# The convolution's bias inside its band matrices, with 62-row window loads; LayerNorm's affine part on VectorE; modulation steps at 0.7 a unit

## The chip, the cores and the metric

The kernel runs on one core of a Trainium2 chip as one program. The core has a matrix engine (TensorE, PE in the profile), a vector engine (VectorE, DVE), an activation engine (ScalarE, ACT), a general engine (GpSimd, POOL), and a queue processor (SyncE, SP) that mostly issues transfers. Sixteen transfer engines move data between the chip's memory and the core's on-chip memory of 128 partitions (rows). Every engine works through its own instruction list in order, and waits on semaphores where an operand is not ready. The metric is the device time of one execution in microseconds.

## What is computed

The reference is one step of a two-layer backbone. 256 prompt tokens and 1024 sample tokens of width 1024 pass an even layer and an odd layer. The change touches the even layer. There the normalised input `h` is multiplied with one wide matrix, and the product is split into a gated convolution branch (`a_u`, `a_g`, `a_z`) and a differential attention branch (`b_q`, `b_k`, `b_v`, `b_z`):

```python
a_u, a_g, a_z, b_q, b_k, b_v, b_z = jnp.split(h @ w_in, SPLIT_E, axis=-1)
a = a_u * jax.nn.sigmoid(a_g)
a = lax.conv_general_dilated(a, conv_w[:, None, :], window_strides=(1,),   # 31 taps, one filter per channel
                             padding=[(15, 15)], ..., feature_group_count=A_W) + conv_b
a = jax.nn.silu(layer_norm(a, ln_g, ln_b)) * jax.nn.silu(a_z)              # A_W = 512 channels
```

`layer_norm` is `(x - mu) * rsqrt(var + 1e-6) * g + b` over the 512 channels. Attention follows with these queries, keys and values, then the output projection of both branches, then the odd layer. Each layer's input is shifted and scaled, and its output gated, by a modulation: `silu(cond) @ w_mod + b_mod`, a matrix of 1024 x 3072 per layer and two conditioning vectors.

## The kernel before

The program runs in stages: the first modulation and the normalised input, the even layer's input projection (`l0_in`, about 50 to 530 us), its attention (`l0_attn`, to about 810), its output projection, and the same for the odd layer.

**The input projection.** `l0_in` goes through seven groups of weight columns, 512 columns each, in the order `ug0`, `ug1` (the gated convolution input), `az`, and heads 0 to 3 (q, k, v and gate of one head each). A group has 10 or 14 units. A unit is 24 matmuls of three products (high and low parts of both sides) over eight slices of 128, into one bank of `acc` (5 buffers), and ends with a function that takes the result out on ACT and DVE and stores it to memory on SP's queue. The next group's eight weight slices (`raw_w`, `w_w`) are loaded in the group's last units, three ahead, cast on ACT and split on POOL (`wcut`).

**The convolution** is a side program, a Python generator `conv()` that `filler` advances by 4/3 steps after each unit. `ug_units` store the gated input, in high and low parts, to the memory tensors `AW` (a plane of rows of tokens per part, 256 channels wide, two buffers `ahl` on the way). For each of eight sets `q` of 64 channels, `windows(q)` (lines 432 to 440) loads `X`: 128 partitions, of which the first 64 hold the high part and the last 64 the low part of 64 successive token rows; 42 such windows with a step of 32 rows; 64 channels. A set takes four transfers, each of 64 rows with 21 pieces of 64 channels (256 bytes), issued on SP. `X` has two buffers, so set `q+2` can be loaded when set `q` has been used. A band matrix per channel (`toep`, two 256 KB loads in flight, cut by `wcut` on DVE) holds the 31 taps shifted 32 times: 64 rows, 32 columns, written twice one under the other. One matmul per channel (line 471, `tr_cv`) gives 42 x 32 output tokens; line 476 (ACT) and 477 (DVE) add the band's two parts into `cy`, and line 480 stores a set's `cy` to `CV` on ACT's queue, 42 rows of 32 pieces of 256 bytes. `AW` holds twice the gated value, so the result is twice the convolution without its bias.

**LayerNorm** follows as the second part of the same side program (`ln_steps`, 0.8 steps a unit), for ten tiles of 128 tokens: DVE halves and adds the bias (line 575), takes mean and variance (577 to 580), POOL raises to the power -1/2 (`rsq`, line 95), DVE makes the offset (582), ACT normalises (587), POOL multiplies by `ln_g` (588) and adds `ln_b` (589), ACT takes tanh (610), DVE applies both gates (593, 594), SP stores to `CAT`.

**The modulation** for later stages is a third side program, `mod_vec` (line 162): 48 steps, each a 256 KB load (`rawm`, two buffers) and two DVE operations of 128x512 that multiply and sum, each with a readout of the sum. `filler` advances it by one step a unit from the second group on.

**What sets the order.** The framework orders the instructions of each engine when the program is built, from the order written and from a model of times; on the chip each engine's list is fixed. `l0_in` calls `freed` six units before the end of the last head: the space of one input half is released, and the keys of attention head 0 and three query blocks are loaded there (`l0_keys`, `l0_query`, four loads of 128 KB each block). All SP transfers go through one hardware queue (q1), ACT's through another (q10), POOL's through a third (q0).

Of the kernel before, what the change touches and what calls it, by code (L numbers as in the profile page):

```python
# [76 lines left out]
class K:  # L77
# [323 lines left out]
    def l0_in(self, ws, raw, wp, cxp, p1, small, acc, pst, mod, freed):  # L401
# [21 lines left out]

        def conv():

# [6 lines left out]
            def windows(q):  # L432
                x = cxp.tile([128, CWIN, CCH], F32R, tag="X", bufs=2, name=f"X{q}")
                cs = slice(q % 4 * CCH, q % 4 * CCH + CCH)
                for o in range(2):
                    for hl in range(2):
                        src = self.AW[q // 4][hl, 32 * o : 32 * o + 32 * CWIN, cs].rearrange("(j r) c -> r j c", r=64)
                        dst = x[hl * 64 : hl * 64 + 64].rearrange("p (j o) c -> p o j c", o=2)[:, o]
                        nc.sync.dma_start(f32(dst), f32(src))
# [43 lines left out]
        def head_units(h):  # L483
# [23 lines left out]
            def vz_done(t, ps):  # L507
                v = small.tile([128, 128], F32, tag="vz", name=f"vz{h}_{t}")
                nc.scalar.copy(v, ps[:, 256:384])
                nc.sync.dma_start(self.V0[h, t], v)  # L510
                gz = small.tile([128, 128], F32, tag="gz", name=f"gz{h}_{t}")
# [45 lines left out]
        def ln_steps():  # L557
# [3 lines left out]
            con = cxp.tile([128, 3, 512], F32, tag="cy", bufs=1, name="lncon")  # L561
            for i, nm in enumerate(("lng", "lnb", "convb")):
                nc.sync.dma_start(con[:, i], a[nm].broadcast_to([128, 512]))
# [9 lines left out]
            def stats(t):  # L573
                u = us[t % 6]
                nc.vector.scalar_tensor_tensor(u, u, 0.5, con[:, 2], ALU.mult, ALU.add)
# [4 lines left out]
                nc.vector.tensor_scalar(mv[:, 1:2], mv[:, 1:2], EPS, None, ALU.add)  # L580
                self.rsq(mv[:, 2:3], mv[:, 1:2])
                nc.vector.tensor_scalar(mv[:, 3:4], mv[:, 0:1], mv[:, 2:3], -1.0, ALU.mult, ALU.mult)

            def norm(t):
                u, mv = us[t % 6], mvs[t]
                nc.sync.dma_start(azs[t % 2], self.AZ[t])
                nc.scalar.activation(u, u, AF.Identity, bias=mv[:, 3:4], scale=mv[:, 2:3])
                nc.gpsimd.tensor_tensor(u, u, con[:, 0], ALU.mult)
                nc.gpsimd.tensor_tensor(u, u, con[:, 1], ALU.add)
# [25 lines left out]
        convd, credit, RATE, LNR = [], [0.0], 4 / 3, 0.8  # L615
# [9 lines left out]
        def filler(rate, mods, at=None):  # L625
# [5 lines left out]
            def f(b):  # L631
# [4 lines left out]
                for _ in range(b):  # L636
# [4 lines left out]
                    for _ in range(mods):  # L641
# [6 lines left out]
            (1, lambda: ug_units(1), tok, filler(RATE, 1)),  # L648
            (6, az_units, tok, filler(RATE, 1)),
            (2, lambda: head_units(0), hd, filler(RATE, 1)),  # L650
            (3, lambda: head_units(1), hd, filler(RATE, 1)),
            (4, lambda: head_units(2), hd, filler(RATE, 1)),
            (5, lambda: head_units(3), [1] * 14, filler(RATE, 1, 6)),
# [929 lines left out]
```

## Time and profile before

| | |
|---|---|
| Median of 3 runs | 1825.25 us (1824.95 to 1827.32) |
| The profiled execution's own time | 1827.64 us |
| Its span, first to last instruction | 1825.9 us |
| PE busy | 1727.1 us (95%) |
| DVE / ACT / POOL busy | 1242.8 / 974.1 / 797.3 us |
| Transfers | 241.24 MB, mean 132 GB/s |
| Convolution matmuls (line 471) | 512 groups, 139.2 to 405.0 us |
| LayerNorm's operations | 423.7 to 499.2 us |
| Granted TensorE clock, mean | 0.985 |

The profile is one execution. The rows of a stage table give, for a stretch of time in us from the span's start, its length, then the busy time (and number of instructions) of PE, PE's weight loads, DVE, ACT and POOL, then the granted TensorE clock, the mean share in which the sixteen transfer engines had packets under way (overlapping packets count twice, so it can be over 1), and GB/s. A row of a wait table names who waited, for whom, the total in us, how often, and the longest. A row of a tile's table gives shortest, median and longest duration in ns, then first and last start in us. A row of the transfer table gives KB of one transfer and the median us from issue to landing.

### The profile page before, as it was taken

The page shows a single profiled execution, that of the slowest core. Times are in us where ns is not written, and L with a number is a line of the kernel's source. Part 1 is how long each engine was busy: PE and PEld are TensorE (multiplying, and loading weights), DVE is VectorE, ACT ScalarE, POOL GpSimd, SP SyncE. Part 2 cuts the span into 40 slices and gives each one's busy share as a digit, 9 for nine tenths or more (in the row PEclk, how much of TensorE's full clock was granted, in tenths as well). Part 3 has the DMA queues.
Part 4 walks back from the last instruction along what each step waited for, and adds up shares of the span by engine and source line. Part 5 has one row for each costly group of instructions (what it writes and reads, how often), then busy time and mean ns, then how long its engine had stood idle before and what let it go on. Part 6 is the DMA issues. An engine that isn't in the chain of part 4 may idle for free. (4 is left out here: it accounts for less than half of the span.)

```text
span 1825.9 us, 28267 instructions
## 1 busy us (share of the span) xinstructions
PE 1727.1 (95%) x9434; PEld 1421.5 (78%) x9434; DVE 1242.8 (68%) x2935; ACT 974.1 (53%) x2060; POOL 797.3 (44%) x716
## 2 busy tenths in 40 slices
PE   6998999998979899999999999998999999999998
PEld 2787788887767677778887778877888888878886
DVE  7656665675859889935576672118999899999322
ACT  6432334443347678743344533227778788898311
POOL 2321032236637777863237873202343334455332
PEclk9999999999989999999999999999999999999999
DMA  8468878865693332144246345254122114141441
GB/s 299 160 157 196 214 208 185 205 178 167 182 254 93 101 100 88 45 138 162 76 158 194 140 132 156 81 141 103 36 57 58 30 41 107 59 137 61 154 172 58
DMA packets 220278, 241.24 MB, mean 132 GB/s; under 512 B 72128, under 2 KB 154848, under 8 KB 219876
## 3 DMA queue, kind: packets, MB, share of 16 engines
q1 hardware_dynamic: 207476, 233.53, 44.2%
q0 software_dynamic: 1792, 3.15, 0.9%
q10 hardware_dynamic: 10864, 2.75, 0.8%
q8 instruction: 75, 1.23, 0.3%
q14 instruction: 71, 0.58, 0.1%
HBM read 169.08 MB, written 70.28 MB: 131 GB/s over the span
## 5 line engine op out<-in xcount | busy, mean ns | idle before, releaser
L397 ACT ACTIVATE E<-E,mm 128x1536 f32<-128x1536 f32 (+3 forms) x240 | 293.1, 1224 | 71.1 <-DVE E L394 61.4
L270 POOL TENSOR_TENSOR w_w<-raw_w,w_w 128x512 fp32r<-128x512 f32 x88 | 122.9, 1406 | 246.3 <-ACT w_w L269 232.8
L1239 PE MATMUL S<-k1d,q1s 128*128 128x512 f32 (+1 forms) x704 | 206.0, 390 | 4.8 <-DVE E L394 2.1
L372 POOL TENSOR_TENSOR el<-ef,eh 128x512 fp32r<-128x512 f32 x96 | 124.1, 1293 | 188.2 <-DVE eh L371 183.3
L394 DVE TENSOR_SCALAR_CACHE_REDUCE E<-S,mm 128x512 f32<-128x512 f32 x256 | 190.0, 744 | 14.8 <-PE S L799 5.2
L1169 PE MATMUL wt_et<-ident,E 128*128 128x128 f32 x1264 | 187.4, 273 | 3.7 <-DVE om L1192 2.3
L1169 PEld LDWEIGHTS wt_et<-ident,E 128*128 128x128 f32 x1264 | 154.8, 141 | 39.2 <-DVE om L1192 2.7
L368 DVE TENSOR_TENSOR el<-wt_et,eh 128x512 fp32r<-128x512 f32 x220 | 147.0, 682 | 8.3 <-ACT eh L367 7.9
L1239 PEld LDWEIGHTS S<-k1d,q1s 128*128 128x128 f32 x704 | 120.3, 190 | 27.2 <-DVE E L394 7.9
L1164 PE MATMUL pv_pv<-el,v 128*128 128x512 f32 x316 | 139.1, 440 | 0.4 <-POOL el L372 0.2
L367 ACT CAST eh<-wt_et 128x512 fp32r<-128x512 f32 x220 | 123.6, 592 | 26.8 <-PE wt_et L1169 26.2
L799 PE MATMUL S<-kd,qs 128*128 128x512 f32 (+1 forms) x416 | 130.0, 426 | 7.6 <-DVE E L394 6.3
L319 PE MATMUL acc_g<-w_w,hi 128*128 128x512 f32 x336 | 132.3, 394 | 0.0
L318 PE MATMUL acc_g<-w_w,hi 128*128 128x512 f32 x336 | 131.5, 393 | 0.8 <-DVE v L1022 0.7
L320 PE MATMUL acc_g<-w_w,lo 128*128 128x512 f32 x336 | 131.7, 392 | 0.0
L1163 PE MATMUL pv_pv<-eh,v 128*128 128x512 f32 x316 | 128.2, 406 | 0.6 <-DVE eh L371 0.3
L874 PE MATMUL acc_po<-wo,oh 128*128 128x512 f32 x320 | 126.2, 396 | 0.3 <-DVE oy L746 0.3
L875 PE MATMUL acc_po<-wo,oh 128*128 128x512 f32 x320 | 125.2, 392 | 0.0
L394 DVE TENSOR_SCALAR_CACHE_REDUCE E<-S 128x512 f32<-128x512 f32 (+1 forms) x160 | 100.1, 630 | 17.3 <-PE S L1239 9.2
L269 ACT CAST w_w<-raw_w 128x512 fp32r<-128x512 f32 x96 | 58.9, 619 | 94.4 <-DMA raw_w<-in_we 29.5
L878 PE MATMUL acc_po<-wo,ol 128*128 128x512 f32 x320 | 103.2, 394 | 0.0
L799 PEld LDWEIGHTS S<-kd,qs 128*128 128x128 f32 x416 | 70.3, 196 | 28.6 <-DVE E L394 20.4
(295 smaller groups left out, 4570.7 us busy)
## 6 DMA issues: line engine op xcount, KB each, us to landing
rawm_v<-in_wmodt SPq DMA_DIRECT2D x64, 256.0 KB, 3.1
raw_w<-in_we SPq DMA_DIRECT2D x56, 256.0 KB, 3.1
X<-AW SPq DMA_DIRECT2D x32, 336.0 KB, 7.1
qs<-QK SPq DMA_DIRECT2D x80, 128.0 KB, 2.8
ac<-CAT SPq DMA_DIRECT2D x20, 512.0 KB, 4.1
raw_w<-in_wod SPq DMA_DIRECT2D x40, 256.0 KB, 2.6
q1s<-qT SPq DMA_DIRECT2D x40, 256.0 KB, 2.6
xraw_m<-in_wmod SPq DMA_DIRECT2D x32, 256.0 KB, 4.4
```

What stands on the lines that cost most here:

```text
L318: nc.tensor.matmul(ps[:, o:], a, w[:, 0, o:], start=(k == 0), stop=False)
L319: nc.tensor.matmul(ps[:, o:], a, w[:, 1, o:], start=False, stop=False)
L320: nc.tensor.matmul(ps[:, o:], b, w[:, 0, o:], start=False, stop=(k == KC - 1))
L368: nc.vector.tensor_tensor(lo, ps, f32(hi), ALU.subtract)
L394: nc.vector.tensor_scalar(e[:, o : o + w], S, -1.0, init, ALU.mult, ALU.min, accum_out=m[:, i : i + 1])
L397: nc.scalar.activation(e[:, :n], e[:, :n], AF.Exp, bias=init, scale=-1.0, accum_out=s)
L799: nc.tensor.matmul(S, q[:, hl], kd[:, c, kofs + o : kofs + o + n], start=(hl == 0), stop=(hl == 1))
L874: nc.tensor.matmul(po[hn], oh[:, k, :], wo[k][:, 0, s], start=(k == 0), stop=False)
L1163: nc.tensor.matmul(pv, vs, wh, start=(i == 0), stop=False)
L1164: nc.tensor.matmul(pv, vs, wl, start=False, stop=(i == nk - 1))
L1169: nc.tensor.transpose(ps[:, g * 128 : g * 128 + 128], E[g][:, ec : ec + 128], self.ident)
L1239: nc.tensor.matmul(S, qs[:, g, :], kd[hl][:, kc : kc + n], start=(hl == 0), stop=(hl == 1))
```

## The change

- **Window loads and the bias.** The two window tiles are allocated once (`win`) and partly filled by POOL: rows 32 to 63 with 2.0 and rows 96 to 127 with 0.0, four fills of 32 x 2688 numbers. The loads then write 62 rows of each half in place of 64, so rows 62 and 63 keep 2.0 and 126 and 127 keep 0.0. Row 62 of every band matrix, zero until now, holds the channel's bias. The matmul so adds twice the bias. The number of loads (32), of their pieces per row (21) and their issuing queue stay.
- **LayerNorm.** Line 575 and the offset of 582 go, since the bias is in, and the factor 2 is left in and met by `4 * EPS`. Normalising and the affine part are two DVE operations: `(u - mean) * g`, then `* rstd + b`. ACT's operation and POOL's two a tile go.
- **Modulation** steps run at 0.7 a unit in place of 1.
- **Buffers.** `vz` and `gz`, a unit's value and gate on their way to memory, get three buffers in place of two.
- **Queries.** One query block of head 0 is loaded ahead in place of three; the others are loaded by the attention stage when it gets to them.

```diff
+        win = [cxp.tile([128, CWIN, CCH], F32R, tag="X", bufs=2, name=f"win{i}") for i in range(2)]
+        for w in win:
+            nc.gpsimd.memset(f32(w[32:64]), 2.0)
+            nc.gpsimd.memset(f32(w[96:128]), 0.0)
...
             def windows(q):
-                x = cxp.tile([128, CWIN, CCH], F32R, tag="X", bufs=2, name=f"X{q}")
+                x = win[q % 2]
                 cs = slice(q % 4 * CCH, q % 4 * CCH + CCH)
                 for o in range(2):
                     for hl in range(2):
-                        src = self.AW[q // 4][hl, 32 * o : 32 * o + 32 * CWIN, cs].rearrange("(j r) c -> r j c", r=64)
-                        dst = x[hl * 64 : hl * 64 + 64].rearrange("p (j o) c -> p o j c", o=2)[:, o]
+                        src = self.AW[q // 4][hl, 32 * o : 32 * o + 32 * CWIN, cs].rearrange("(j r) c -> r j c", r=64)[0:62]
+                        dst = x[hl * 64 : hl * 64 + 62].rearrange("p (j o) c -> p o j c", o=2)[:, o]
                         nc.sync.dma_start(f32(dst), f32(src))
...
-                v = small.tile([128, 128], F32, tag="vz", name=f"vz{h}_{t}")
+                v = small.tile([128, 128], F32, tag="vz", bufs=3, name=f"vz{h}_{t}")
...
-                gz = small.tile([128, 128], F32, tag="gz", name=f"gz{h}_{t}")
+                gz = small.tile([128, 128], F32, tag="gz", bufs=3, name=f"gz{h}_{t}")
...
             def stats(t):
                 u = us[t % 6]
-                nc.vector.scalar_tensor_tensor(u, u, 0.5, con[:, 2], ALU.mult, ALU.add)
...
-                nc.vector.tensor_scalar(mv[:, 1:2], mv[:, 1:2], EPS, None, ALU.add)
+                nc.vector.tensor_scalar(mv[:, 1:2], mv[:, 1:2], 4 * EPS, None, ALU.add)
                 self.rsq(mv[:, 2:3], mv[:, 1:2])
-                nc.vector.tensor_scalar(mv[:, 3:4], mv[:, 0:1], mv[:, 2:3], -1.0, ALU.mult, ALU.mult)
...
             def norm(t):
...
-                nc.scalar.activation(u, u, AF.Identity, bias=mv[:, 3:4], scale=mv[:, 2:3])
-                nc.gpsimd.tensor_tensor(u, u, con[:, 0], ALU.mult)
-                nc.gpsimd.tensor_tensor(u, u, con[:, 1], ALU.add)
+                nc.vector.scalar_tensor_tensor(u, u, mv[:, 0:1], con[:, 0], ALU.subtract, ALU.mult)
+                nc.vector.scalar_tensor_tensor(u, u, mv[:, 2:3], con[:, 1], ALU.mult, ALU.add)
...
-        convd, credit, RATE, LNR = [], [0.0], 4 / 3, 0.8
+        convd, credit, RATE, LNR, MR = [], [0.0, 0.0], 4 / 3, 0.8, 0.7
...
-                    for _ in range(mods):
+                    credit[1] += mods
+                    while credit[1] >= 1:
+                        credit[1] -= 1
                         next(mod, None)
...
-                pre.extend([[p], k.l0_keys(0, p, 1), {g: k.l0_query(0, g, p, 3) for g in (1, 2, 0)}])
+                pre.extend([[p], k.l0_keys(0, p, 1), {1: k.l0_query(0, 1, p, 1)}])
...
+    band[:, 62] = i["a_conv_b"][0][:, None]
```

The order of SP's transfers at the first window sets, before (a number behind a name is a buffer's; `x4` is four instructions alike; `AW<-ahl` are stores of the second group's units, `rawm` loads of the modulation, `rawb` loads of bands):

```order
L261 DMA rawm_v_2_5_0_1416<-in_wmodt 128x512
L439 DMA X_1135<-AW_73 64x21x64 x4
L439 DMA X_1281<-AW_73 64x21x64 x2
L420 DMA AW_74<-ahl_2_1131 128x2x256
L439 DMA X_1281<-AW_73 64x21x64
L420 DMA AW_74<-ahl_3_1184 128x2x256
L439 DMA X_1281<-AW_73 64x21x64
L261 DMA rawm_v_2_6_0_1481<-in_wmodt 128x512
```

And there in the change:

```order
L261 DMA rawm_v_2_4_0_1539<-in_wmodt 128x512
L445 DMA win_739<-AW_73 62x21x64 x4
L445 DMA win_740<-AW_73 62x21x64 x4
L263 DMA raw_w_0_1476<-in_we 128x512
L263 DMA raw_w_1_1478<-in_we 128x512
L263 DMA raw_w_2_1480<-in_we 128x512
L261 DMA rawm_v_2_5_0_1602<-in_wmodt 128x512
L261 DMA rawm_v_2_6_0_1722<-in_wmodt 128x512
L420 DMA AW_74<-ahl_2_1137 128x2x256
L420 DMA AW_74<-ahl_3_1178 128x2x256
```

The eight loads of the first two sets now stand together; the stores of units 2 and 3, which stood among them, come behind them, with three weight slices and two modulation loads in between.

SP at the third window set, in the change (before, the set stood at the same place, with `raw_w_5` and one band load among its four):

```order
L263 DMA raw_w_4_1508<-in_we 128x512
L445 DMA win_739<-AW_73 62x21x64 x4
L263 DMA raw_w_5_1522<-in_we 128x512
L263 DMA rawb_band_1590<-in_toep 128x512
L261 DMA rawm_v_0_7_0_2422<-in_wmodt 128x512
L261 DMA rawm_v_1_0_0_2539<-in_wmodt 128x512
L263 DMA raw_w_6_1554<-in_we 128x512
L263 DMA raw_w_7_1568<-in_we 128x512
```

The last three weight slices of the next group (`az`) stand behind the set, as do the next band and two modulation loads.

VectorE at the start of LayerNorm, before:

```order
L575 SCALAR_TENSOR_TENSOR lnw_4291<-lnw_4291,lncon 128x512
L340 SCALAR_TENSOR_TENSOR gz_5_4391<-th_z_5_4392,acc_v_5_4363 128x128
L577 BN_STATS bn_4399<-lnw_4291 128x6
L575 SCALAR_TENSOR_TENSOR lnw_4291<-lnw_4291,lncon 128x512
L513 TENSOR_TENSOR gz_5_4391<-gz_5_4391,subg 128x128
L579 BN_AGGR mv_4401<-bn_4399 128x2
```

And in the change, a little further on, where the first modulation operation stands among LayerNorm's:

```order
L592 SCALAR_TENSOR_TENSOR lnw_4189<-lnw_4189,mv_4357,lncon 128x512
L584 BN_AGGR mv_4457<-bn_4455 128x2
L584 BN_AGGR mv_4505<-bn_4503 128x2
L597 SCALAR_TENSOR_TENSOR lnw_4189<-lnw_4189,lnw_4190 128x512
L162 ISA md_v_1_2_1_0_4775,modv_1_1184<-rawm_v_1_2_1_4773,cr(0, 2)_1_3255 128x512
L162 ISA modv_1_1184 128x1
L500 TENSOR_TENSOR ch_2_1_4346<-cn_2_1_4392,ropeT 128x512
```

Before, the last modulation operation stood ahead of LayerNorm's first. Now twelve of them stand between its first statistics and its last store, and the two DVE operations of the affine part stand where ACT's and POOL's results were awaited.

More of the change, by code (lines that the diff above doesn't have):

```diff
@@ L557, in ln_steps @@
         def ln_steps():
-            con = cxp.tile([128, 3, 512], F32, tag="cy", bufs=1, name="lncon")
-            for i, nm in enumerate(("lng", "lnb", "convb")):
+            con = cxp.tile([128, 2, 512], F32, tag="cy", bufs=1, name="lncon")
+            for i, nm in enumerate(("lng", "lnb")):
                 nc.sync.dma_start(con[:, i], a[nm].broadcast_to([128, 512]))
@@ L647, in l0_in @@
             (0, lambda: ug_units(0), [4, 1, 1, 1, 3], filler(0, 0)),
[L648 to L653, printed above, removed]
+            (1, lambda: ug_units(1), tok, filler(RATE, MR)),
+            (6, az_units, tok, filler(RATE, MR)),
+            (2, lambda: head_units(0), hd, filler(RATE, MR)),
+            (3, lambda: head_units(1), hd, filler(RATE, MR)),
+            (4, lambda: head_units(2), hd, filler(RATE, MR)),
+            (5, lambda: head_units(3), [1] * 14, filler(RATE, MR, 6)),
         ]
@@ L1524, in _layout @@
         band[:, m : m + 31, m] = i["a_conv_w"][0].T
+    band[:, 62] = i["a_conv_b"][0][:, None]
     band = band.reshape(32, 16, 64, 32).transpose(0, 2, 1, 3).reshape(32, 64, 512)
     z["toep"] = c(np.concatenate([band, band], 1))
-    z["convb"] = c(i["a_conv_b"])
     z["lng"], z["lnb"] = c(i["a_ln_g"]), c(i["a_ln_b"])
```

## The prediction

> **What bounds the kernel now.** I read the page's first part, then one row of the stage table for the stretch in which the convolution's windows are loaded, then the waits of TensorE in that stretch.
>
> ```profile
> span 1825.9 us, 28267 instructions
> PE 1727.1 (95%) x9434; PEld 1421.5 (78%) x9434; DVE 1242.8 (68%) x2935; ACT 974.1 (53%) x2060; POOL 797.3 (44%) x716
> 128.00:352.00 224.00, 216.45 (x1334) 184.79 (x1333) 141.04 (x294) 80.41 (x183) 46.19 (x30) 0.99 0.84 199
> PE tr_cv L471 <- DVE cy L477: 6.0, 4, 4.0
> PE tr_cv L471 <- DMA X<-AW: 1.9, 1, 1.9
> ```
>
> The kernel is TensorE's: 1727.1 of 1825.9 us, and 216.45 of the 224 us in which it works on the projection and the convolution together. In that stretch it waited 1.9 us, once, for a window (`X<-AW`, columns: time, times, longest). The windows are free now. But the transfer engines are 0.84 busy there, so nothing says that they stay free when they get slower.
>
> **The window loads: how many engines carry one.** This is the edit that decides. Each of the 32 loads moved 64 rows (partitions) of 21 pieces of 256 B; now it moves 62 rows. I looked up in the transfer table on how many of the 16 engines loads with odd numbers of rows ran.
>
> ```profile
> DMA packets 220278, 241.24 MB, mean 132 GB/s; under 512 B 72128, under 2 KB 154848, under 8 KB 219876
> q0 software_dynamic: 1792, 3.15, 0.9%
> q10 hardware_dynamic: 10864, 2.75, 0.8%
> X<-AW SPq DMA_DIRECT2D x32, 336.0 KB, 7.1
> CV<-cy ACTq DMA_DIRECT2D x8, 336.0 KB
> AW<-z SPq DMA_DIRECT2D x2, 98.0 KB
> AW<-z SPq DMA_DIRECT2D x2, 30.0 KB, 3.6
> qn<-in_qn SPq DMA_DIRECT2D x1, 32.0 KB
> modc<-in_bmodc SPq DMA_DIRECT2D x4, 4.0 KB, 3.1
> ```
>
> Queue q10 carries only the eight stores `CV<-cy` of 42 rows by 32 pieces of 256 B, 10,752 packets; 10,864 were counted. The other 112 are 14 a store: one closing packet from each engine that took part. So 42 rows ran on 14 engines, three rows each. Two rules fit that: only equal shares are dealt out (14 is the largest divisor of 42 up to 16), or shares are rounded up (three rows each, until they run out). For 62 rows the first gives 2 engines with 31 rows each, the second 16 engines with four or fewer.
>
> The page's count of short packets separates them. Of 72,128 under 512 B, 43,008 are window pieces (32 x 64 x 21), 10,752 are `CV` pieces, 256 belong to `qn` and `kn`, 256 to `cc` and `bcol`, and 1,280 to the ten 4 KB column loads like `modc`. That leaves 16,576 closing packets. SP issues 1,016 transfers (all its counts in the issue table), ACT 8, POOL 16; 16 apiece would be 16,640. So 64 are missing. The `CV` stores miss 16. Two transfers of 2 rows (`condr`) miss 28, two of 15 rows (the 30 KB `AW<-z`) miss 2. The last 18 must be the two 49-row transfers (98 KB: 49 rows of two 1 KB pieces): 9 missing each, 7 engines. With shares rounded up these would use 13 engines and miss 6 in all. 7 is the largest divisor of 49 up to 16: equal shares it is, and a 62-row load runs on **two engines**.
>
> The Trainium skill has this as a rule: "DMA: Bandwidth & Descriptors", section "Why a DMA increments its semaphore by 16 and not by 1", says that a hardware-queue transfer uses the largest number of engines up to 16 that divides the outermost size of both sides. It speaks against this change; the trace agrees, with 14 for 42 rows and 7 for 49.
>
> **What one load then costs.** Each of the two engines moves 31 x 21 = 651 pieces of 256 B instead of 84.
>
> ```profile
> 130.00:132.00 2.00, 2.00 (x10) 1.60 (x9) 2.00 (x8) 0.97 (x3) 0.00 (x0) 1.00 1.24 215
> 134.00:136.00 2.00, 2.00 (x11) 1.59 (x10) 0.00 (x0) 0.00 (x0) 0.00 (x0) 1.00 1.38 171
> 530.00:540.00 10.00, 8.18 (x24) 5.11 (x24) 9.02 (x27) 7.28 (x10) 2.71 (x3) 0.83 1.10 326
> 127.93 9.45 SPq L439 DMA_DIRECT2D X<-AW  x6
> 141.86 0.58 SPq L439 DMA_DIRECT2D X<-AW  x1
> 172.22 5.68 SPq L439 DMA_DIRECT2D X<-AW  x3
> 353.36 2.01 SPq L439 DMA_DIRECT2D X<-AW  x2
> ```
>
> The last figure of a stage row is GB/s over 16 engines. Windows alone are in flight at 130 (215 GB/s, one engine 13.4, 19.1 ns a piece) and at 134 (171 GB/s, 24.0 ns). By queue q10, 0.8% of 16 x 1825.9 us over 10,864 packets is 21.5 ns. Below all of these lies the rate for large pieces at 530, 326 GB/s: 20.4 GB/s an engine would be 12.5 ns. Two engines load memory far less than sixteen, so I take 20 ns, near the 19.1 row. Four loads make a window set, and all four use the same two engines: 4 x 651 x 20 ns = **52.1 us a set** (49.7 at 19.1, 62.5 at 24, 32.6 at 12.5), where it was 4 x 84 x 20 ns = 6.7 us.
>
> **What waits for it.** There are eight sets, the first two issued together at 127.93 to 141.86, each later one when the set before last has been consumed (172.22 is the third). Every SP transfer that is spread over the engines has a sixteenth on each of the two busy ones, behind the window pieces in the same queue. The order of SP shows weights, the `AW` stores, `rawm` and band loads right behind each set; none of them finishes before it. TensorE goes on until it needs one of these. The stores' tiles (`ahl`, `az`, `ch`) have two buffers, so I let it run two units.
>
> ```profile
> 412.57 0.39 PE L330 MATMUL acc_c<-hi,w_w 128*128 128x512 f32 x1
> 418.07 0.39 PE L330 MATMUL acc_c<-hi,w_w 128*128 128x512 f32 x1
> ```
>
> The two rows are 24 matmuls apart, one unit: 5.5 us, two are 11.0. The first pair of sets adds 2 x 52.1 - 11.0 = 93.2 us, each of the other six 52.1 - 11.0 = 41.1, together 246.6. Sum **+340 us**. As a cross-check, the busiest engine's own work: 8 x 52.1 = 417 us of windows; the rest of the stretch is 199 GB/s x 224 us = 44.6 MB, less 30 windows (10.3 MB) and six `CV` stores (2.1 MB), 32.2 MB, a sixteenth at 20.4 GB/s 99 us, and 11 us for `CV`. That is 527 us for what took 233 (127.93 until the last set lands 7.1 us after 354): at least +294.
>
> **The other edits.** They meet in the LayerNorm stage and are small beside this.
>
> ```profile
> 430.00:440.00 10.00, 3.80 (x16) 2.65 (x15) 10.00 (x20) 4.57 (x10) 9.29 (x7) 0.77 0.14 33
> 450.00:460.00 10.00, 6.88 (x37) 5.55 (x36) 8.07 (x10) 3.59 (x9) 10.00 (x8) 0.96 0.67 211
> 500.00:520.00 20.00, 14.66 (x83) 13.24 (x83) 5.49 (x12) 5.50 (x24) 5.05 (x4) 0.83 0.95 257
> PE acc_v L318 <- DVE gz L340: 5.5, 1, 5.5
> L588 POOL TENSOR_TENSOR lnw<-lnw,lncon x10: 1262/1736/1747, 431.2 to 483.6; 128x512 f32<-128x512 f32 x10
> L587 ACT ACTIVATE lnw<-lnw,mv x10: 804/816/827, 429.9 to 481.9; 128x512 f32<-128x512 f32 x10
> L593 DVE SCALAR_TENSOR_TENSOR lnw<-lnw,lnw x9: 682/1573/1784, 436.4 to 493.5; 128x512 f32<-128x512 f32 x9
> L162 DVE CUSTOM_DVE_ANT_0 md_v<-rawm_v,cr(0, 2)_1_2586 x48: 680/700/1784, 218.1 to 395.6; 128x512 f32<-128x512 f32 x48
> L405 POOL MEMSET z<- x1: 515/515/515, 0.9 to 0.9; 64x512 f32 x1
>   DMA GZ<-gz: 6.6, 4
> ```
>
> TensorE idles 6.2, 3.1 and 5.3 us in the three rows, 14.6 us, the most that can be won here. One wait of 5.5 us is on `gz`, which stands on VectorE behind LayerNorm's work. VectorE's own 128x512 operation takes 682 ns alone and 1573 in the middle, where POOL is 9.3 to 10 of 10 us busy. POOL loses 20 operations (ten at 1.7 us; the ten of line 589 are like them), ACT ten of 0.82 us, VectorE gains ten of 0.68 less ten small ones, some 5 us. The third buffers of `vz` and `gz` take away the 6.6 us that VectorE waited for `GZ` stores, on a busy engine four times. Against it stand 12 modulation operations at 0.70 us, 8 us, which the order of VectorE puts into the LayerNorm rows. I take -8 for these (bounds -15 and 0). The four fills of the window tiles are 32x2688 on POOL, no row shows one; by `z` (512 columns in 515 ns) 2.7 us each, 0 to 10.8. I take 0, since they stand before the windows' wait and POOL is empty there (0.00 in the rows at 130 and 134). The queries: eight loads fewer before the attention, the same eight behind its start, 0 (-5 to 5).
>
> Sum: 340 - 8 = +332 on the profiled span of 1825.9; that execution took 1827.6, 2.4 us over the median of the runs, so 1825 + 332 = **2157 us**.
>
> **The rivals.**
>
> A, as above: two engines, partly covered. Range 2085 (the engine's own work at 19.1 ns a piece, +275, less 15) to 2240 (24 ns a piece, 83 us more). Chance 0.62.
>
> B, nothing is covered: VectorE's next modulation operation or band cut waits for a load behind the windows, and the convolution's own evictions (`cy`) stand behind it, so TensorE stops at once. For it: `DVE cy` is already what TensorE waits for most in this stretch (6.0 us). Against it: two band and two `rawm` loads are in hand at any time. At 24 ns: 8 x 62.5 = 500, less 8: 2317 us. Chance 0.20.
>
> C, the two engines are quicker when alone: 12.5 ns, as for large pieces. For it: 215 GB/s falls to 171 when more windows are in flight, so something shared limits sixteen engines. Against it: small pieces cost more per byte in every row here. 93.2 becomes 54.2 and 41.1 becomes 21.6: +184 - 8, 2001 us. Chance 0.12.
>
> D, 62 rows still run on 16 engines, some with a row less; then the windows are 3% smaller and only the small edits count: 1825 - 8 = 1817 us, faster. It decides if this path deals rows out differently from the 49-row transfers. Against it: the closing packets. Chance 0.05. Something else: 0.01.
>
> **How the numbers follow.** 2157 is A's time. The range 2000 to 2340 takes in A and most of B and C; D and their edges are left out. A measurement of this kernel can tell about 0.2% from no change. Only D is not slower: faster 0.04, same 0.01, slower 0.95.
>
> **What would show it.** In the new profile the loads `win<-AW` should land some 50 us after issue or later, not 7. TensorE should stand idle some 330 us more, nearly all between 130 and 700 us, released by transfers or by VectorE and ACT operations that waited for transfers; the share of busy transfer engines there should fall from 0.84 to below 0.5. Queue q1's packets should fall by 32 x 42 pieces and 32 x 14 closing packets. Attention and the second layer should keep their lengths to some 5 us. If the windows still land in under 15 us, D holds. If the sets land in 33 us, C; if TensorE does nothing while a set is in flight, B. In the LayerNorm stage POOL should be less than half as busy and VectorE's operations nearer to 0.68 us.

## The result, and the profile after

| | before | after |
|---|---|---|
| Median of 4 runs, us | 1825.78 (1824.95 to 1827.32) | 2031.48 (2029.30 to 2038.96) |
| Ratio of the runs | | 1.1123, interval 1.1104 to 1.1141 |
| Profiled execution, us | 1827.64 | 2029.30 |

The change makes the kernel about 206 us slower. The forecast was 2157 us, 332 us slower, with a range from 2000 to 2340 us. The measured time is in the range, but below the 2085 to 2240 us that the prediction's own account, A, gave, and nearest to the 2001 us of its rival C.

The first view is the page of the changed kernel: the span, the busy time of the engines, TensorE's busy tenths in 40 slices of 50.7 us, and the main transfer queue.

```profile
span 2027.5 us, 28257 instructions
PE 1743.0 (86%) x9434; PEld 1431.5 (71%) x9434; DVE 1217.8 (60%) x2935; ACT 964.5 (48%) x2050; POOL 775.6 (38%) x700
PE   6963665673958989999999989999899999999998
q1 hardware_dynamic: 205540, 232.92, 38.0%
```

TensorE is at 3 to 7 tenths from the third slice to the tenth and in the twelfth (101 to 608 us), and at 8 or 9 from then on. Queue q1 has 1,936 packets fewer: 32 x 42 pieces, 32 x 14 closing packets, and 144 that belong to the load of the bias vector that is gone (128 pieces and 16 closing packets). The first two terms are those that the prediction named for loads on two engines.

The next view is the table by stage, before (first fence) and after (second). The first row of each is the whole stretch from the first window load to attention's first matmul, the second lies inside the convolution, and the third runs from the last convolution matmul to attention.

```profile
128.00:526.00 398.00, 373.71 (x2310) 323.99 (x2309) 256.51 (x512) 144.90 (x357) 128.15 (x91) 0.97 0.77 194
172.00:405.00 233.00, 226.47 (x1476) 196.86 (x1475) 152.41 (x314) 92.38 (x219) 56.47 (x38) 0.99 0.82 201
405.00:526.00 121.00, 105.10 (x615) 92.64 (x615) 75.32 (x135) 40.17 (x112) 65.40 (x50) 0.92 0.66 184
```

```profile
124.00:737.00 613.00, 397.45 (x2319) 340.38 (x2318) 244.64 (x516) 137.46 (x349) 98.25 (x72) 0.81 0.45 126
230.00:623.00 393.00, 244.63 (x1474) 210.10 (x1473) 132.39 (x274) 91.18 (x219) 54.09 (x38) 0.79 0.40 113
623.00:737.00 114.00, 103.25 (x600) 90.50 (x600) 83.28 (x179) 33.19 (x101) 37.88 (x31) 0.94 0.73 210
```

The stretch grew from 398 to 613 us, by 215; it starts about 3 us earlier, and attention behind it is 10 us shorter. TensorE's idle time in it grew from 24.3 to 215.6 us, by 191, and its busy time by 24. In the middle rows nearly the same number of matmuls (1,476 and 1,474) takes 393 us in place of 233, while the transfer engines fall from 0.82 to 0.40 busy. The last rows went the other way, from 121 to 114 us.

What the two engines do is seen at the first sets, in rows of 5 us of the changed kernel.

```profile
140.00:145.00 5.00, 0.00 (x0) 0.00 (x0) 0.00 (x0) 0.00 (x0) 0.00 (x0) 0.50 0.16 36
160.00:165.00 5.00, 0.12 (x2) 0.15 (x3) 0.00 (x0) 0.00 (x0) 0.00 (x0) 0.50 0.16 36
165.00:170.00 5.00, 5.00 (x28) 4.11 (x28) 2.30 (x4) 1.95 (x4) 0.00 (x0) 0.63 0.16 36
170.00:175.00 5.00, 5.00 (x33) 4.20 (x32) 0.00 (x0) 0.96 (x2) 0.00 (x0) 1.00 0.15 33
```

At 140 us no engine of the core does anything. The transfer engines move 36 GB/s at a share of 0.16 of sixteen, which is 2.5 engines' worth, as overlapping packets count twice. The rows of the kernel before at 130 and 134 us had 215 and 171 GB/s. 36 GB/s over two engines is 18 GB/s an engine, 256 bytes in **14.2 ns**. The prediction had taken 20 ns. A set is 4 x 651 x 14.2 ns = 37.0 us, not 52.1. The rows also show the granted clock: 0.50 in the last 5 us of the idle time, 0.63 in the first 5 us of work after it, then 1.00.

The waits of TensorE (first fence, 100 to 760 us) and of VectorE (second, 100 to 620 us) in the changed kernel:

```profile
PE tr_cv L477 <- DVE cy L483: 122.1, 15, 26.2
PE acc_az L318 <- ACT w_w L269: 30.0, 1, 30.0
PE tr_cv L477 <- DMA win<-AW: 29.8, 1, 29.8
PE acc_c L330 <- ACT w_w L269: 24.8, 3, 19.2
```

```profile
DVE md_v L162 <- DMA rawm_v<-in_wmodt: 106.4, 13, 36.4
DVE cy L483 <- ACT cy L482: 104.6, 21, 33.0
DVE band_band L270 <- ACT band_band L269: 79.5, 7, 26.5
```

Only 29.8 us of TensorE's waits, one wait, are for a window itself. The rest are for weights (`w_w`) and for `cy`, and VectorE in turn waits for modulation loads (`rawm`) and for band cuts whose raw data stands behind the windows. So the windows delay what is queued behind them, and this reaches TensorE over VectorE and ACT. The first two stalls, in rows of TensorE's and VectorE's timelines (in brackets the idle time before the instruction, and what ended it):

```profile
164.88 0.78 PE L477 MATMUL tr_cv<-band_band,win 128*42 128x64 f32 x8 [29.83 <-DMA win<-AW]
205.21 0.70 DVE L162 CUSTOM_DVE_ANT_0 md_v<-rawm_v,cr(0, 2)_0_1185 128x512 f32<-128x512 f32 x1 [36.43 <-DMA rawm_v<-in_wmodt]
205.83 0.66 DVE L483 TENSOR_TENSOR cy<-tr_cv,cy 42x256 f32<-42x256 f32 x1
206.54 0.81 PE L477 MATMUL tr_cv<-band_band,win 128*42 128x64 f32 x8 [26.24 <-DVE cy L483]
```

The first stall ends with the first window set itself. The second ends with a modulation load: VectorE has waited 36.4 us for it, then adds into `cy`, and only then can TensorE go on.

One row of the window tile, and one of SyncE's timeline, show something more: SyncE itself is held up.

```profile
L445 SPq DMA_DIRECT2D win<-AW x32: 251/9073/14189, 124.5 to 571.2; - x32
L426 POOL MEMSET win<- x2: 2337/2338/2340, 109.2 to 114.0; 32x2688 f32 x2
L427 POOL MEMSET win<- x2: 2337/2340/2342, 111.6 to 116.4; 32x2688 f32 x2
124.55 66.52 SPq L445 DMA_DIRECT2D win<-AW  x8
```

Issuing one window load takes 9.07 us in the median, and the first eight take 66.5 us together; 651 pieces at 14.2 ns are 9.2 us. So SyncE's issuing keeps step with the two engines. It runs ahead of them by about one load: the eighth is issued by 191.1 us, and in the trace's records of packets the last piece of the eight has moved at 201.8 us. In the kernel before, the median was 0.78 us:

```profile
L439 SPq DMA_DIRECT2D X<-AW x32: 579/779/3404, 127.9 to 354.0; - x32
```

The four fills take 2.34 us each and end at 118.7 us, before the first load.

LayerNorm's operations on VectorE after the change (lines 591 and 592 are the two new ones, 596 the gate that was line 593):

```profile
L591 DVE SCALAR_TENSOR_TENSOR lnw<-lnw,mv,lncon x10: 731/739/1718, 643.1 to 690.7; 128x512 f32<-128x512 f32 x10
L592 DVE SCALAR_TENSOR_TENSOR lnw<-lnw,mv,lncon x10: 731/742/1527, 645.0 to 695.8; 128x512 f32<-128x512 f32 x10
L596 DVE SCALAR_TENSOR_TENSOR lnw<-lnw,lnw x9: 647/675/1776, 647.6 to 698.9; 128x512 f32<-128x512 f32 x9
```

The gate's median fell from 1573 to 675 ns, and POOL is busy for 37.9 of 114 us there in place of 65.4 of 121. That the one follows from the other is not shown: with the affine part back on ACT and POOL (an experiment below) POOL is busy for 65.5 of 125 us, and the gate's median is 682 ns all the same.

### The profile page after: what moved, and what is told of

The parts are those of the page before. It is cut to its first block, busy times and chain, and to the rows that moved or that the text cites. A ratio compares the mean times of both kernels' runs of the same rounds, so it can differ in the third digit from the quotient of the medians.

```text
span 2027.5 us, 28257 instructions
## 1 busy us (share of the span) xinstructions
PE 1743.0 (86%) x9434; PEld 1431.5 (71%) x9434; DVE 1217.8 (60%) x2935; ACT 964.5 (48%) x2050; POOL 775.6 (38%) x700
## 5 line engine op out<-in xcount | busy, mean ns | idle before, releaser
L477 PE MATMUL tr_cv<-band_band,win 128*42 128x64 f32 x512 | 47.4, 241 | 152.0 <-DVE cy L483 122.1
L477 PEld LDWEIGHTS tr_cv<-band_band,win 128*42 128x42 f32 x512 | 46.0, 166 | 160.0 <-DVE cy L483 116.0
L367 ACT CAST eh<-wt_et 128x512 fp32r<-128x512 f32 x220 | 124.4, 596 | 30.6 <-PE wt_et L1174 30.1
## 6 DMA issues: line engine op xcount, KB each, us to landing
win<-AW SPq DMA_DIRECT2D x32, 325.5 KB
```

## The experiments

Two theories stand against each other from the start. The one of the prediction: the number of engines that carry a load is the largest divisor of its rows up to 16, and the number of pieces on each sets the time. The rival: something else in the change (the fixed tiles and their fills, the moved modulation steps, the new order of the units, the bias row) makes the convolution wait. All differences below are against the changed kernel, or against the 63-row version where that is said.

The table gives the stages of every profiled execution: time of the first convolution matmul, of the last, then the lengths up to attention's first matmul, up to the output projection, and from there to the end (from the first and last starts of `tr_cv`, `S<-kd,qs` and `acc_po`). For the changed kernel these are the rows it is read from, with the first and last start behind the three durations:

```profile
L477 PE MATMUL tr_cv<-band_band,win x512: 191/240/284, 164.9 to 622.8; 128*42 128x64 f32 x171
L804 PE MATMUL S<-kd,qs x416: 274/397/766, 737.4 to 982.6; 128*128 128x512 f32 x128, 128*128 128x256 f32 x11
L879 PE MATMUL acc_po<-wo,oh x320: 387/389/481, 1001.8 to 2018.6; 128*128 128x512 f32 x160
```

| version | first conv | last conv | to attention | attention | rest | span |
|---|---|---|---|---|---|---|
| before | 139.2 | 405.0 | 120.8 | 274.6 | 1025.5 | 1825.9 |
| after | 164.9 | 622.8 | 114.6 | 264.4 | 1025.7 | 2027.5 |
| 64 rows | 136.2 | 411.5 | 114.1 | 263.8 | 1024.9 | 1814.3 |
| 48 + 14 rows | 140.0 | 413.5 | 112.0 | 267.8 | 1032.2 | 1825.5 |
| 63 rows | 137.5 | 408.4 | 111.7 | 267.9 | 1026.8 | 1814.8 |
| 57 rows | 148.6 | 502.0 | 115.2 | 268.2 | 1026.5 | 1911.9 |
| 61 rows | 198.0 | 894.5 | 113.5 | 267.9 | 1025.6 | 2301.5 |
| bias edit alone | 165.0 | 627.2 | 117.4 | 274.1 | 1030.1 | 2048.8 |
| 62 rows, POOL's queue | 195.2 | 778.4 | 111.9 | 268.4 | 1026.5 | 2185.2 |
| 63 rows, affine back | 137.9 | 407.3 | 124.7 | 265.3 | 1025.5 | 1822.8 |
| 63 rows, three queries | 137.0 | 407.9 | 113.6 | 273.7 | 1030.3 | 1825.5 |
| 63 rows, steps at 1 | 137.3 | 411.7 | 113.2 | 270.0 | 1026.8 | 1821.7 |
| 63 rows, two buffers | 136.7 | 411.1 | 111.0 | 268.2 | 1026.6 | 1816.9 |

### 64 rows again

```diff
-  ...rearrange("(j r) c -> r j c", r=64)[0:62]
+  ...rearrange("(j r) c -> r j c", r=64)[0:64]
...
```

All else of the change stays. Tokens overwrite the constant in rows 62 and 63, so the bias is not added as it should be.

> The change with window loads of 64 rows again (the fills' rows 62 and 63 are overwritten by tokens, so the bias is left out of the result; all else of the change stays). Theory T, two engines carry a 62-row load and everything on SP's queue stands behind it: 64 rows run on 16 engines, the 218 us that the convolution's stretch gained are gone, and the 16 us won in the LayerNorm stage and the attention stay: 1809 to 1816 us. Rival R, the stretch is long because of the fills, the moved modulation steps or the new order on VectorE: it stays over 1950 us.

Measured: 1818.74 us over 10 runs, ratio to before 0.9964 (0.9947 to 0.9982). Queue q1 has 207,332 packets, 32 x 42 pieces and 32 x 14 closing packets more than with 62 rows. The whole stall is gone, with the fills, the modulation rate and the order of the change in place. The rival falls. The time is 3 us above the range that was expected.

### The same 62 rows in two pieces

```diff
...
-  nc.sync.dma_start(f32(dst), f32(src))
+  for r0, r1 in ((0, 48), (48, 62)):
+      dst = x[hl * 64 + r0 : hl * 64 + r1].rearrange("p (j o) c -> p o j c", o=2)[:, o]
+      nc.sync.dma_start(f32(dst), f32(src[r0:r1]))
...
```

> The change with each 62-row load cut into one of 48 rows and one of 14 (16 and 14 engines by equal shares), result as the reference's. T: per engine a set is 4 x (63 + 21) pieces as before the change, 32 more issues on SP of 0.33 us beside 224 us of TensorE's work: 1809 to 1818 us, closing packets 32 x (16 + 14). R, or rows are dealt out rounded up and something else is slow about a row count that is no power of two: over 1900 us.

Measured: 1823.27 us over 12 runs, ratio 0.9983 (0.9965 to 1.0). The same bytes, the same 62 rows and the same constant rows, in twice as many loads, and the stall is gone; the packets are 32 x 28 more (206,436), 16 and 14 engines in place of 2. So it is neither the bytes nor the bias row. The time is 5 us above what was expected. Against the 63-row version of the next experiment the table has the convolution's end 5.1 us later and the stages from the output projection on 5.4 us longer (1032.2 us against 1026.8). This edit changes nothing in those stages; why they are longer stays open.

### 63 rows

```diff
-  ...rearrange("(j r) c -> r j c", r=64)[0:62]
+  ...rearrange("(j r) c -> r j c", r=64)[0:63]
...
-    band[:, 62] = i["a_conv_b"][0][:, None]
+    band[:, 63] = i["a_conv_b"][0][:, None]
```

The constant is now in row 63 alone; row 62 meets a zero in the band, as before.

> The change with 63-row loads and the bias in row 63 of the bands, result as the reference's. One row more. T: 63 rows run on 9 engines (7 rows each), a set is 4 x 147 pieces an engine, at 14.1 to 24 ns 8 to 14 us, about what TensorE runs on meanwhile: 1809 to 1820 us, closing packets 32 x 9. Rival: any row count other than 64 falls back to few engines or to a slow path: over 1950 us.

Measured: 1811.27 us over 6 runs, ratio 0.9916 (0.9892 to 0.9941): **15 us under the kernel before (0.8%), 220 us under the change**, the lowest median of this study; the version with two buffers, below, can't be told apart from it. One row more, a number that 16 does not divide either, and no stall. Queue, matmuls, the stretch, and 2 us at the first loads of the 63-row version:

```profile
q1 hardware_dynamic: 206436, 233.09, 42.6%
L477 PE MATMUL tr_cv<-band_band,win x512: 191/239/274, 137.5 to 408.4; 128*42 128x64 f32 x171
128.00:360.00 232.00, 222.63 (x1366) 190.45 (x1365) 133.60 (x273) 83.90 (x189) 44.52 (x30) 0.98 0.71 195
129.00:131.00 2.00, 2.00 (x10) 1.64 (x9) 0.42 (x1) 0.60 (x2) 0.00 (x0) 1.00 0.68 146
```

Against the changed kernel q1 has 896 packets more: 32 x 21 pieces and 32 x 7 closing packets, so nine engines where there were two, and 63 = 9 x 7. TensorE is busy 222.6 of 232 us. Nine engines are enough. At 129 us only window pieces and their closing packets are in the trace's records, at 146 GB/s: 16.2 GB/s for each of nine engines, 15.8 ns a piece.

### 61 rows

```diff
-  ...rearrange("(j r) c -> r j c", r=64)[0:62]
+  ...rearrange("(j r) c -> r j c", r=64)[0:61]
...
```

Row 61 keeps the constant, so the last tap of the last of the 32 outputs of a window is left out and twice its weight added in its place.

> The change with 61-row loads (row 61 of the window keeps the constant, so the last tap row is left out of the result). One row fewer. T: 61 is prime, one engine, 1281 pieces of 14.1 ns, 72.3 us a set; by the chain (two sets less 11 us, six sets less 11 us each) 134 + 368 = 501 us in the convolution's stretch where the change has 218, so 2031 + 284 = 2315 us (2270 to 2350). Rival, the load's cost goes with its bytes: no difference to the change, 2025 to 2035 us.

Measured: 2305.2 us, ratio 1.2618 (1.257 to 1.2666), within the range. A stretch of the first sets, and SyncE's issue of them:

```profile
140.00:145.00 5.00, 0.00 (x0) 0.00 (x0) 0.00 (x0) 0.00 (x0) 0.00 (x0) 0.50 0.08 18
124.03 127.22 SPq L445 DMA_DIRECT2D win<-AW  x8
L477 PE MATMUL tr_cv<-band_band,win x512: 192/241/287, 198.0 to 894.5; 128*42 128x64 f32 x171
```

18 GB/s in all, and 204,836 packets, 32 x 21 pieces and 32 closing packets less than the change: one engine at the rate that each of the two had. One row less than the change costs another 274 us.

### 57 rows

```diff
-  ...rearrange("(j r) c -> r j c", r=64)[0:62]
+  ...rearrange("(j r) c -> r j c", r=64)[0:57]
...
```

Rows 57 to 61 keep the constant, so the taps that fall on them meet it in place of tokens.

> The changed kernel with windows loaded 57 rows at a time; rows 57 to 61 of the taps hold the constant instead, so that five of the 49 + 13 tap rows' values are left out of the result. Theory (rows go in equal shares to the largest number of engines up to 16 that divides them): 57 is 3 x 19, so three engines with 399 pieces each, 5.6 us a load at the 14.1 ns measured in the changed kernel, a set of four 22.5 us, eight sets 180 us less some 77 us beside TensorE's runs, +103 us on a version without the stall (1811 us): about 1914 us, 1890 to 1940. Rival 1 (an odd number of rows is what costs, or any number that 16 does not divide): as slow as 62 rows, about 2030 us. Rival 2 (rows are dealt out almost evenly over all engines whenever there are more than a few rows over): about 1811 us.

Measured: 1913.67 us in one run, beside 1822.54 for the kernel before on the same chip. The theory had said 1914. That it is met this closely is luck in part, as it took 77 us of the loads to be covered by TensorE's work, and the table gives 88 (worked out further below). Both rivals fall: fewer rows than in the change, an odd number, and some 115 us faster (1.050 of before in place of 1.1123).

Queue, a stretch of the first sets, and SyncE's issue of the window loads:

```profile
q1 hardware_dynamic: 202212, 232.06, 39.9%
140.00:145.00 5.00, 0.00 (x0) 0.00 (x0) 0.00 (x0) 0.00 (x0) 0.00 (x0) 0.50 0.24 54
123.87 39.95 SPq L445 DMA_DIRECT2D win<-AW  x8
L445 SPq DMA_DIRECT2D win<-AW x32: 259/5588/8563, 123.9 to 448.6; - x32
```

54 GB/s is three times 18. The queue's packets are those of the change less 32 x 5 x 21 pieces, plus 32: one closing packet more a load, three engines. With 57, 62 and 61 rows an engine has 399, 651 and 1281 pieces, and the eight first loads keep SyncE for 40.0, 66.5 and 127.2 us.

### The bias edit alone

The kernel before, with the edit on windows and bias only:

```diff
+        win = [cxp.tile([128, CWIN, CCH], F32R, tag="X", bufs=2, name=f"win{i}") for i in range(2)]
...
-                        src = ....rearrange("(j r) c -> r j c", r=64)
+                        src = ....rearrange("(j r) c -> r j c", r=64)[0:62]
...
-                nc.vector.scalar_tensor_tensor(u, u, 0.5, con[:, 2], ALU.mult, ALU.add)
-                nc.vector.tensor_scalar(mv[:, 1:2], mv[:, 1:2], EPS, None, ALU.add)
+                nc.vector.tensor_scalar(mv[:, 1:2], mv[:, 1:2], 4 * EPS, None, ALU.add)
...
+    band[:, 62] = i["a_conv_b"][0][:, None]
```

> The kernel before with the bias put into its bands and the windows loaded 62 rows at a time, and nothing else of the change (LayerNorm's affine part, modulation steps, queries and buffers as before). Theory (the piece count of the window loads alone makes the slowdown): eight sets at 36.8 us, of which about 77 us in all lie beside two units' TensorE runs, so about 218 us more in the convolution; the small gains of the other edits are missing, so 2035 to 2046 us. Rival (the slowdown needs the moved modulation steps or the new order of the units as well): below 1950 us.

Measured: 2050.83 us, ratio 1.1248 (1.1215 to 1.128), 5 us over the range. The last convolution matmul starts 222 us later than before. So this edit does not need the others to make the slowdown, and the others together hide 0.0125 of 1825 us, some 23 us of it (1.1248 against 1.1123, with intervals that don't overlap). By the table, against the change: 4.4 us later at the convolution's end, 2.8 in the LayerNorm stage, 9.7 in attention, 4.4 behind it.

### The windows on GpSimd's queue

```diff
-                        nc.sync.dma_start(f32(dst), f32(src))
+                        nc.gpsimd.dma_start(f32(dst), f32(src))
```

> The changed kernel with the 32 window loads of 62 rows issued by GpSimd on its own queue instead of SyncE's; all else as it is. Theory 1 (the rule of equal shares belongs to the engines and holds for every queue): the loads still run on two engines, 36.8 us a set, but no longer ahead of SyncE's transfers on the same queue; eight sets are 294 us of the two engines, and the convolution cannot be faster than that, so over 1900 us. Theory 2 (the rule belongs to SyncE's kind of queue): the loads run on all engines, land in about 10 us or less, and the time is that of the version without the stall, 1811 to 1830 us, the upper part if GpSimd's issuing takes its time from its own work.

Measured: 2187.03 us in one run, 1.200 of before in place of the change's 1.1123, some 160 us more. The window tile, GpSimd's timeline, then the transfers between 160 and 178 us (GB/s in 40 slices of 0.45 us, packets, and the one load of that stretch):

```profile
L445 POOL DMA_DIRECT2D win<-AW x32: 4004/4008/4242, 124.4 to 724.7; - x32
160.06 4.00 POOL L445 DMA_DIRECT2D win<-AW  x1 [12.10 <-issue]
178.27 4.01 POOL L445 DMA_DIRECT2D win<-AW  x1 [14.20 <-issue]
195.40 4.01 POOL L445 DMA_DIRECT2D win<-AW  x1 [13.12 <-issue]
GB/s 0 0 0 0 0 0 0 0 0 0 20 5 22 49 22 22 23 14 30 32 23 22 40 24 21 21 51 23 22 22 37 37 36 36 46 46 36 34 6 0
DMA packets 672, 0.37 MB, mean 21 GB/s; under 512 B 590, under 2 KB 590, under 8 KB 672
win<-AW POOLq DMA_DIRECT2D x1, 325.5 KB, 17.9
```

Theory 2 falls: a load does not land in 10 us. Theory 1's bound holds, but it does not name what sets this time. Here a load is issued only when the one before has landed: issued at 160.06, landed 17.9 us later, the next issued at 178.27. The first four take 71 us, from 124.4 to 195.4, where the two engines on SyncE's queue needed 37. The load is still cut in two: of its 672 packets 82 are over 2 KB and carry the 325.5 KB, and in the trace's records two of the 82 have 2816 bytes and 80 have 4096, twice 40 x 4096 + 2816 = 651 x 256 bytes. The other 590 are 574 packets of 64 or 44 bytes and 16 closing packets of 4, so on this queue closing packets do not count the engines that carry the data. The Trainium skill, "DMA: Bandwidth & Descriptors", section "Why a DMA increments its semaphore by 16 and not by 1", gives the rule of the largest divisor for both kinds of queue, and names an exception: on trn2 some direct copies from GpSimd's queue get 16 engines with rounded-up shares. This load is not one of those; with four rows an engine it would have 16 short ends, not two. Of the 17.9 us, 4.0 are GpSimd's issue, in which nothing moves (the first slices), and the data then take some 13 us in place of 9.2. Why they move more slowly there, and why the next load waits for the one before, stays open.

### Which of the small edits pays

Four runs each take one edit back out of the 63-row version. LayerNorm's affine part on ACT and POOL again:

```diff
+                nc.vector.tensor_scalar(mv[:, 3:4], mv[:, 0:1], mv[:, 2:3], -1.0, ALU.mult, ALU.mult)
...
-                nc.vector.scalar_tensor_tensor(u, u, mv[:, 0:1], con[:, 0], ALU.subtract, ALU.mult)
-                nc.vector.scalar_tensor_tensor(u, u, mv[:, 2:3], con[:, 1], ALU.mult, ALU.add)
+                nc.scalar.activation(u, u, AF.Identity, bias=mv[:, 3:4], scale=mv[:, 2:3])
+                nc.gpsimd.tensor_tensor(u, u, con[:, 0], ALU.mult)
+                nc.gpsimd.tensor_tensor(u, u, con[:, 1], ALU.add)
```

> The 63-row version with LayerNorm's affine part on ACT and POOL again. Theory L, freeing POOL is what shortened the stretch from the last convolution matmul to the first attention matmul (111.7 us in the 63-row run, 120.8 before): it goes back to 118 us or more, the whole to 1815 to 1820 us. Rival: the gain is the other small edits'; then this is within 3 us of the 63-row version.

Measured: 1825.99 us, ratio 0.9996 (0.998 to 1.0012); the stage up to attention is 124.7 us in place of 111.7. The edit takes 13 us off this stage, and the whole is 6 us above the expected range. That it is POOL's time that counts, as that theory says, is not told apart from ACT's, since the edit gives work back to both.

Three queries ahead again:

```diff
-  pre.extend([[p], k.l0_keys(0, p, 1), {1: k.l0_query(0, 1, p, 1)}])
+  pre.extend([[p], k.l0_keys(0, p, 1), {g: k.l0_query(0, g, p, 3) for g in (1, 2, 0)}])
```

> The 63-row version with three query blocks loaded ahead again. Theory Q, the attention is shorter (267.9 us in the 63-row run, 274.6 before) because fewer loads stand before its keys: the attention goes back to 272 us or more and the whole to 1815 to 1819 us. Rival: the attention's 7 us come from VectorE's and POOL's new order, and the whole stays within 3 us; or the queries loaded late cost there (2.8 us of waits on qs) and this is 2 to 3 us faster.

Measured: 1825.47 us, ratio 0.9985 (0.9969 to 1.0). Attention takes 273.7 us in place of 267.9, as expected. The whole is 6 us above the expected range; 3.5 us more are in the stages behind, which the theory does not explain.

Modulation steps at one a unit again:

```diff
-        convd, credit, RATE, LNR, MR = [], [0.0, 0.0], 4 / 3, 0.8, 0.7
+        convd, credit, RATE, LNR, MR = [], [0.0, 0.0], 4 / 3, 0.8, 1.0
```

> The 63-row version with a modulation step a unit again. If the twelve operations moved into LayerNorm cost what they take, the last convolution matmul comes later by some 3 us (more work on VectorE beside the convolution) and the stretch behind it shorter by up to 8: 1806 to 1812 us. Rival: spreading the steps is what gains, by fewer waits for cy in the convolution: the convolution's end moves from 408 to 412 us or later and the whole is 1815 us or more.

Measured: 1824.87 us, ratio 0.9986 (0.9965 to 1.0008). The convolution ends 3.3 us later, at 411.7, and attention is 2.1 us longer. TensorE's waits for `cy` from 120 to 415 us, first in this run, then in the 63-row version:

```profile
PE tr_cv L477 <- DVE cy L483: 9.0, 6, 2.6
PE tr_cv L477 <- DVE cy L483: 3.3, 4, 1.8
```

The theory of that expectation falls, and the rival fits, though the convolution's end just misses its 412 us: the lower rate pays.

Two buffers for `vz` and `gz` again:

```diff
-  v = small.tile([128, 128], F32, tag="vz", bufs=3, name=f"vz{h}_{t}")
+  v = small.tile([128, 128], F32, tag="vz", name=f"vz{h}_{t}")
-  gz = small.tile([128, 128], F32, tag="gz", bufs=3, name=f"gz{h}_{t}")
+  gz = small.tile([128, 128], F32, tag="gz", name=f"gz{h}_{t}")
```

> The 63-row version with two buffers for vz and gz again. Before the change VectorE waited 6.6 us for GZ stores and ACT 4.0 for V stores; TensorE waited for none of them directly. If they matter through what stands behind: 1813 to 1817 us. Rival: nothing, within 2 us of the 63-row version.

Measured: 1813.99 us, ratio 0.9932 (0.9906 to 0.9958), not to be told apart from the 63-row version; whether the buffers are worth 2 us or nothing stays undecided.

Taken one by one, the first three edits are worth 0.0080, 0.0069 and 0.0070 of the time, 14.6, 12.6 and 12.8 us, each to some 5 us. Together they would be 40 us, but all edits together gain 15.3. So they do not add up: with any one of them out, nearly the whole gain is gone. The 63-row version ran on another chip than these four, each beside the kernel before; against the two-buffer version, which ran on their chip, the three are worth 11.7, 9.7 and 9.9 us, and still do not add up. Why, no run shows. The stages place part of it (13 us up to attention, 6 in attention, 3 and 2 for the modulation), from one profiled execution each.

## Why the prediction was right, and where its numbers were off

**The rule of equal shares: right.** Two engines for 62 rows was read from closing packets of the profile before. The packet counts of six row counts agree (64, 63, 62, 61, 57, and 48 with 14), and the three that use few engines move 18, 36 and 54 GB/s. Rival D, sixteen engines, fell.

**The price of a piece: the term that was mis-sized.** The step "two engines load memory far less than sixteen, so I take 20 ns" drew the wrong conclusion from its own first half. The runs show 14.2 ns on one, two and three engines, between rival C's 12.5 ns and the 19.1 ns row, and nearer to C's. C's reason, that the engines are quicker when few work, is borne out: 14.2 ns on one to three engines, 15.8 on nine, 19.1 and 24.0 on sixteen. Its size, the price of large pieces, is not. The rows at 130 and 134 had shown where to look: 215 GB/s fell to 171 with more windows in flight. What the sixteen share, no run shows. A set is 37.0 us in place of 52.1.

**The chain: near in size with the measured price, but its cover has another reason.** First pair 2 x 37.0 - 11.0 = 63.0, six times 37.0 - 11.0 = 156.0, together +219 in place of +340. The convolution's end gives the same from the other side: against the 63-row version it moved by 214.4 us in the change, by 93.6 with 57 rows and by 486.1 with 61. Eight sets of the moved pieces are 296, 181 and 582 us, so 81, 88 and 96 us of them were covered, against 7 x 11 = 77 taken for the cover of two units a set. B's size, nothing covered, falls with this: it would have 296 us. But the reason that the prediction gave for the 11 us, two buffers for the tiles of the stores, is not what stopped TensorE. At the first pair it stopped at 135.1 us, 10.5 us after the first window load was issued, and for the window itself; at the second it stopped for `cy`. That the cover comes out near 77 us is luck as far as these runs show.

**Who waits: right in that all stands behind the windows, but the main path is rival B's.** "None of them finishes before it" was said of what stands behind the windows, and holds. Of the 206.7 us in the four rows of TensorE's waits 29.8 are for windows, 54.8 for weights, as A has it, and 122.1 for `cy`. There a modulation operation or band cut of VectorE waits for a load behind the windows, and the convolution's evictions stand behind that operation, as B said. So B's path carries the larger part, at near A's cover. What the prediction did not have: SyncE keeps only about one load ahead of the two engines, so the transfers behind a set are issued late as well.

**TensorE's idle time: too large in the forecast** by the same term, 191 us more in place of 330. 24 of the stretch's 215 us are not idle time. By the trace TensorE is busy for 65.2 us of the stretch at a granted clock of 0.50, against 16.6 before. Its matmuls start 0.43 us apart at 167.6 us, at that clock, and 0.23 us apart at 169.1, at the full one, so about half of the 48.6 us more is lost, which is the 24. The sum had no term for that; the 81 to 96 us of cover above are already less this loss.

**The other edits: right in sign, too small.** -8 was taken, with bounds -15 and 0. Without the stall (63 rows) they are worth -15.3 us (-19.7 to -10.8), at the bound. POOL and VectorE were named: VectorE's gate did go to 0.68 us, and POOL's share there fell from 0.54 to 0.33, which is not "less than half". The run with the affine part put back shows that this edit shortens the stage; it does not show that the gate's speed does. The fills are 2.34 us, estimated 2.7, and hidden, as taken.

**"Attention keeps its length to some 5 us": wrong.** It went from 274.6 to 264.4 us; the step that failed is "the queries, 0 (-5 to 5)". Three queries ahead cost attention 5.8 us in the run that puts them back, and the rest of the 10 is not traced to one edit. The second layer kept its length (1025.7 against 1025.5).

**The sum with the measured terms:** 219 - 15 = +204, against +201.6 in the spans and +206 in the medians.

**What it named as signs:** the share of busy transfer engines fell to 0.45 and the packets of q1 as said. No landing time of the windows is given by the page of the changed kernel, but TensorE's wait for the first set ended at 164.88 us, 40 us after its first load was issued. That lies between the 33 us that were to show C and the 50 that were to show A. And the row at 140 us, in which TensorE does nothing while a set is in flight, is the sign that was to show B. The signs alone would not have picked A.

## What to carry to other kernels

Before the rows of a transfer are changed, find the largest divisor of their number up to 16: 62 rows ran on two engines, 61 on one, 57 on three, 63 on nine, and 64 on sixteen. A cheap remedy is to move a row that isn't needed (63) or to cut the load so that each part divides well (48 and 14). On SyncE's and ACT's queues here the closing packets in a profile's packet counts tell how many engines a transfer used, before anything is changed (on GpSimd's there are 16 a load whatever carries the data); and the price of a piece should be taken from a row with as few engines at work as there will be.

## What was not expected of the hardware

- One transfer engine moves 256-byte pieces at 18 GB/s, 14.2 ns a piece, whether it works alone or with one or two others; on nine an engine had 16.2 GB/s, and with the windows of the kernel before on sixteen 10.7 to 13.4.
- SyncE is held up by a backlog on a few engines: the median issue of a window load went from 0.78 us before to 5.6 us (57 rows) and 9.1 us (62 rows), each the time of one load on its engines. With 61 rows on one engine the median was 8.8 us, not the 18.2 us of a load, but the first eight took 127.2 us. Every transfer behind them then waits to be issued.
- GpSimd's queue took these loads one at a time, 15 to 22 us each, so moving a slow load out of SyncE's way made the kernel slower.
- The stalls of TensorE cost more than their length: in the first 5 us of work behind the first one the granted clock is 0.63, and over the whole stretch this makes some 24 us.
